# One Trainium2 core, a hybrid decoder block: the last chunk of y_b kept on chip and merged first, with its loads and splits in another order

## The chip, the core and the metric

The kernel runs on one core of a Trainium2 chip. TensorE (PE) multiplies, VectorE (DVE), ScalarE (ACT) and GpSimd (POOL) do elementwise work, and SyncE (SP) issues most of the transfers. Each engine takes its instructions in the order in which they were written for it, and waits at the first one whose data is not there. The metric is the device time of one execution in microseconds (us): the median of three runs of the kernel before is 2276.87 us (2275.35 to 2277.63).

## The reference

For an input x of 2048 positions by 1024 channels the block computes, in float32:

```
q, k, v, g_attn, u_lru, g_lru, gate_logits = split(x @ w_in + b_in)
y_a = (attention over 3 dilated head groups * silu(g_attn)) @ w_attn_proj
h   = rg_lru(conv(u_lru));   y_b = (h * silu(g_lru)) @ w_lru_proj
merged = sigmoid(gA) * y_a + sigmoid(gB) * y_b
out = layer_norm(2**0.25 * x + merged @ w_out + b_out)
```

The three attention groups are combined per head by their softmax denominators before the gate. Each product is made of three float32r products of split operands (high*high, high*low, low*high), so every operand is split into a rounded part (ACT) and a remainder (DVE, sometimes POOL) before PE reads it.

## The kernel before

All of w_in is multiplied first, then the attention runs. The change touches only what follows, from about 1792 us to the end. In that part the 2048 positions are four chunks of 512 columns (`c`), and the 1024 channels are eight blocks of 128 rows (`f`, `k`).

**y_b.** `yb_job(n)`, n = 0 to 31, goes through the chunks in order, eight output blocks each. One product is 24 matmuls of 128x512 (eight k, three products each). VectorE multiplies the result with its gate (`gB`, loaded by `load_gb` one product ahead) and SyncE stores it to DRAM (`yb_scr`). Around each product the loop places other work: the splits of w_lru_proj (`prep_wl`), of the next chunk's h (`load_h`, one block of the next chunk per product, so its block 7 is loaded in a chunk's last product and split in the next chunk's first), of w_attn_proj in the last chunk (`prep_wa`), and parts of W_out (`prep_wo`, 16 halves `(k, j)`: four at n = 16 to 19, four at n = 28 to 31).

**The combination.** `combine(c, hp)` joins the three attention groups for one chunk and one pair of heads: three loads (`oc`), weights on VectorE and ScalarE two products later, norms on VectorE and five tensor operations on GpSimd three products later, and four transposes on TensorE (`ctp`, one PSUM buffer) five products later, whose result VectorE multiplies into `ga`; it is stored to `at_scr`. The table `cmb` says behind which product each of the 16 stands: behind products 3 to 25, chunk 0 first.

**y_a and the output.** `ya_job(i)` multiplies the combined attention by w_attn_proj: 12 matmuls. VectorE multiplies the result with its gate (`gA`), and GpSimd adds the reloaded y_b (`ybr`) into `ME[c]`; both were loaded by `load_ya` two products ahead. The gates have three buffers (`gt`), so the load of gate i+3 waits until the addition of product i has read gate i. `out_job(tt)` multiplies 128 merged positions by W_out (two halves of 24 matmuls) and does the layer norm. It needs the split of `ME[c]`, which `split_m` makes, in three pieces for the first tile. The first eight y_a products carry the last eight halves of W_out, two with each of the products 0 to 3: each half is loaded behind its product and split (`later(1, ...)`) ahead of the next product's evacuation. After them come output tiles and y_a products of the next chunk in turn.

`later(lag, fn)` puts work off by so many products, and `run(late)` at a product's start writes what is due. Buffers are named slots: Z0 to Z2 and X0 to X5 of 16 KB per partition, `rc` six and `gt` three of 2 KB.

Of the kernel before, what the change touches and what calls it, by code (L numbers as in the profile page):

```python
# [15 lines left out]
P = 128  # L16
S = 2048
D = 1024
# [13 lines left out]
def hybrid_block_kernel(ctx: ExitStack, tc: tile.TileContext, a: dict, out: bass.AP):  # L32
# [1127 lines left out]
    GB = {}  # L1160

    def load_gb(n):
        c, f = divmod(n, 8)
        GB[n] = gt(f"gB{n}")
        sp.dma_start(GB[n], mg_scr[D + f * P:D + (f + 1) * P, c * CH:(c + 1) * CH])

    def yb_job(n):
        c, f = divmod(n, 8)
        cs = slice(c * CH, (c + 1) * CH)
        run(late)  # L1170
        if n + 1 < 32:
            load_gb(n + 1)
        yb = fp.tile([P, CH], F32, tag="y", name=f"yb{c}{f}", bufs=4)
        for k in range(8):
            xx = HH[c, k]
            pe.matmul(yb, WL[f][:, 0, k], xx[:, 0], start=(k == 0), stop=False)  # L1176
            pe.matmul(yb, WL[f][:, 0, k], xx[:, 1], start=False, stop=False)  # L1177
            pe.matmul(yb, WL[f][:, 1, k], xx[:, 0], start=False, stop=(k == 7))  # L1178
            if k == 3:
                run(pe_late)  # L1180
        gb = GB.pop(n)
        dve.scalar_tensor_tensor(out=gb, in0=gb, scalar=1.0, in1=yb, op0=ALU.add, op1=ALU.mult)
        later(1, lambda: sp.dma_start(yb_scr[f * P:(f + 1) * P, cs], gb))
        now["n"] += 1

    load_gb(0)
    for n in range(32):
        c, f = divmod(n, 8)
        if n < 6:
            prep_wl(n + 2)  # L1190
        if c + 1 < NCH:
            load_h(c + 1, f)
        else:
            prep_wa(f)
        if 16 <= n < 20 or n >= 28:
            prep_wo(*wo.pop(0))
        if 27 <= n < 31:
            load_at(0, n - 27)
        yb_job(n)
        if n in cmb:  # L1200
            combine(*cmb[n])
# [6 lines left out]


    vx_p = ctx.enter_context(tc.tile_pool(name="vx_p", bufs=1, reuse_waits="tile"))  # L1210
    vec = []
    for j in range(3):
        t = vx_p.tile([P, D], F32, name=f"vec{j}")
        sp.dma_start(t, a["vecs"][j:j + 1, :].broadcast_to([P, D]))
        vec.append(t)
    epst = cst.tile([P, 1], F32, name="epst")
    dve.memset(epst, EPS)

    ME, YG, XR, MS = {}, {}, {}, {}

    def load_ya(i):
        c, f = divmod(i, 8)
        cs = slice(c * CH, (c + 1) * CH)
        YG[i] = gt(f"gA{i}"), rc(f"ybr{i}")
        sp.dma_start(YG[i][0], mg_scr[f * P:(f + 1) * P, cs])
        sp.dma_start(YG[i][1], yb_scr[f * P:(f + 1) * P, cs])

    def ya_job(i):
        c, f = divmod(i, 8)
        if i + 2 < 32:  # L1230
            load_ya(i + 2)
        ga, yb = YG.pop(i)
        ya = fp.tile([P, CH], F32, tag="y", name=f"ya{c}{f}", bufs=4)
        for k in range(4):
            xx = AT[c][:, k]
            pe.matmul(ya, WA[f][:, 0, k], xx[:, 0], start=(k == 0), stop=False)
            pe.matmul(ya, WA[f][:, 0, k], xx[:, 1], start=False, stop=False)
            pe.matmul(ya, WA[f][:, 1, k], xx[:, 0], start=False, stop=(k == 3))
        if f == 0:
            ME[c] = big(("Z0", "Z1")[c % 2], [P, 8, CH], F32, f"me{c}")  # L1240
        dve.scalar_tensor_tensor(out=ga, in0=ga, scalar=1.0, in1=ya, op0=ALU.add, op1=ALU.mult)
        pool.tensor_tensor(out=ME[c][:, f], in0=ga, in1=yb, op=ALU.add)  # L1242

    def load_xr(tt):
        XR[tt] = vx_p.tile([P, D], F32, tag="x", name=f"x{tt}", bufs=3)
# [2 lines left out]
    def split_m(tt, ks=slice(0, 8)):  # L1248
        c, b = divmod(tt, 4)
        m = ME[c][:, ks, b * P:(b + 1) * P]  # L1250
        if ks.start == 0:
            MS[tt] = tuple(vx_p.tile([P, 8, P], F32R, tag=t, name=f"{t}{tt}", bufs=2) for t in ("mh", "ml"))
        mh, ml = (t[:, ks] for t in MS[tt])
        act.activation(mh, m, AF.Copy)
        dve.tensor_tensor(out=ml, in0=m, in1=flat(mh), op=ALU.subtract)

    def out_job(tt):
# [5 lines left out]
        for hf in range(2):  # L1263
# [5 lines left out]
                pe.matmul(z, mh[:, k], w[:, 1, hs], start=False, stop=False)  # L1269
                pe.matmul(z, ml[:, k], w[:, 0, hs], start=False, stop=(k == 7))  # L1270
            zz.append(z)
        if tt + 1 < 16:
            load_xr(tt + 1)
            split_m(tt + 1)
# [39 lines left out]
    def bring_at(c):  # L1314
        for k in range(4):
            if c < NCH:
                load_at(c, k)
        now["n"] += 1

    bring_at(1)  # L1320
    for tt in range(16):
        c, b = divmod(tt, 4)
        run(late)
        out_job(tt)
        if c + 1 < NCH:
# [64 lines left out]
```

## Time and profile before

| what | us |
|---|---|
| median of three runs (lowest, highest) | 2276.87 (2275.35, 2277.63) |
| the profiled execution's own time | 2272.4 |
| span of the profile | 2270.6 |
| first y_b matmul | 1792.1 |
| first y_a matmul | 1983.5 |
| first output matmul | 2013.5 |
| last output matmul | 2261.5 |

The profile is of one execution. Its page has the busy time of each engine, the span in 40 slices with the granted TensorE clock, the chain of work that ended last and the costliest groups of instructions. Its trace can be asked for stretches of time, for who waited for whom, and for single instructions with the idle time in front of them and what ended it. TensorE is busy for 98% of the span, so an edit shows in the time only where TensorE stands still.

### The profile page before, as it was taken

The page shows a single profiled execution, that of the slowest core. Times are in us where ns is not written, and L with a number is a line of the kernel's source. Part 1 is how long each engine was busy: PE and PEld are TensorE (multiplying, and loading weights), DVE is VectorE, ACT ScalarE, POOL GpSimd, SP SyncE. Part 2 cuts the span into 40 slices and gives each one's busy share as a digit, 9 for nine tenths or more (in the row PEclk, how much of TensorE's full clock was granted, in tenths as well). Part 3 has the DMA queues.
Part 4 walks back from the last instruction along what each step waited for, and adds up shares of the span by engine and source line. Part 5 has one row for each costly group of instructions (what it writes and reads, how often), then busy time and mean ns, then how long its engine had stood idle before and what let it go on. Part 6 is the DMA issues. An engine that isn't in the chain of part 4 may idle for free.

```text
span 2270.6 us, 33643 instructions
## 1 busy us (share of the span) xinstructions
PE 2218.0 (98%) x11032; PEld 1869.3 (82%) x11032; DVE 1748.2 (77%) x3244; ACT 1209.9 (53%) x2161; POOL 821.6 (36%) x606
## 2 busy tenths in 40 slices
PE   8999999999999999999999999989999999989998
PEld 6888888888887888888888888889999877767786
DVE  7888898899888786877888877656666578747677
ACT  5456566666565566766677677556666411221100
POOL 1555455455543001201201200476766156421220
PEclk9999999999999999999999999999999999999999
DMA  6977987977977666666766856996977588764431
GB/s 209 261 230 223 264 234 232 259 225 247 262 236 261 210 192 205 212 181 198 221 198 198 230 174 203 264 243 160 261 181 174 177 278 289 255 209 158 157 121 65
DMA packets 307358, 485.84 MB, mean 214 GB/s; under 512 B 90432, under 2 KB 131424, under 8 KB 302576
## 3 DMA queue, kind: packets, MB, share of 16 engines
q1 hardware_dynamic: 278192, 441.80, 63.1%
q0 software_dynamic: 9888, 17.90, 4.9%
q10 hardware_dynamic: 19104, 23.99, 3.4%
q8 instruction: 88, 1.44, 0.3%
q14 instruction: 86, 0.70, 0.1%
HBM read 305.27 MB, written 178.32 MB: 213 GB/s over the span
## 4 chain that ended last, share of the span: by engine, by line
PE 80%; issue 5%; DMA 5%; DVE 5%; POOL 3%; ACT 2%; SPq 1%; ACTq 0%; DVEq 0%; POOLq 0%
PE q L614 58%; PE o L988 4%; PE s L949 3%; PE yb L1177 2%; PE yb L1178 2%; PE yb L1176 2%; PE pt L964 2%; PE z L1270 1%; PE z L1269 1%; PE z L1268 1%; DMA A<-qh_scr 1%; POOL me L1242 1%; PE vtp L366 1%; DMA ybr<-yb_scr 1%; POOL C L797 1%
## 5 line engine op out<-in xcount | busy, mean ns | idle before, releaser
L614 PE MATMUL q<-xT,hS 128*128 128x512 f32 x1632 | 504.0, 390 | 1.4 <-DVE y L230 1.4
L614 PE MATMUL q<-xB,hA 128*128 128x512 f32 x1344 | 417.4, 392 | 9.5 <-ACT xB L218 8.8
L614 PE MATMUL q<-xT,l 128*128 128x512 f32 x1088 | 423.6, 389 | 0.0
L614 PE MATMUL q<-xB,l 128*128 128x512 f32 x944 | 368.4, 390 | 0.0
L614 PEld LDWEIGHTS q<-xT,hS 128*128 128x128 f32 x1632 | 305.3, 188 | 64.8 <-issue 1.8
L614 PEld LDWEIGHTS q<-xB,hA 128*128 128x128 f32 x1344 | 252.3, 189 | 62.9 <-ACT xB L218 8.8
L614 PEld LDWEIGHTS q<-xT,l 128*128 128x128 f32 x1088 | 204.2, 188 | 42.6
L955 ACT ACTIVATE p<-p,osb 128x256 f32<-128x256 f32 (+1 forms) x384 | 156.4, 454 | 112.4 <-DVE osb L953 109.2
L614 PEld LDWEIGHTS q<-xB,l 128*128 128x128 f32 x944 | 177.7, 188 | 37.2
L953 DVE CUSTOM_DVE_ANT_0 p<-s,mask 128x256 f32<-128x256 f32 (+1 forms) x384 | 125.3, 364 | 97.2 <-PE s L949 63.0
L230 POOL TENSOR_TENSOR sw<-sw,sin 128x512 f32<-128x512 f32 x96 | 154.6, 1632 | 122.6 <-ACT sw L318 99.8
L230 POOL TENSOR_TENSOR y<-y,h 128x512 f32<-128x512 f32 x28 | 40.3, 1440 | 413.7 <-DVE h L517 292.6
L988 PE MATMUL o<-V,ptb 128*128 128x65 f32 x1200 | 165.7, 276 | 9.5 <-ACT ptb L969 7.5
L988 PEld LDWEIGHTS o<-V,ptb 128*128 128x128 f32 x1200 | 152.7, 195 | 20.8 <-ACT ptb L969 18.2
L614 PE MATMUL q<-xB,hS 128*128 128x512 f32 x544 | 168.6, 391 | 0.3 <-DVE v L230 0.3
L614 PE MATMUL q<-xT,hA 128*128 128x512 f32 x544 | 168.2, 390 | 0.1
L274 ACT ACTIVATE hA<-wA 128x512 fp32r<-128x512 f32 x220 | 138.8, 635 | 21.2 <-PE g L483 6.6
L274 ACT ACTIVATE hS<-S 128x512 fp32r<-128x512 f32 x170 | 108.5, 638 | 63.8 <-DVE S L230 56.6
L230 POOL TENSOR_TENSOR l<-wA,hA 128x512 fp32r<-128x512 f32 x68 | 108.5, 1596 | 80.8 <-ACT hA L274 59.2
L949 PE MATMUL s<-B,A 128*128 128x256 f32 (+1 forms) x384 | 116.2, 325 | 4.1 <-DMA A<-qh_scr 2.1
L614 PEld LDWEIGHTS q<-xT,hA 128*128 128x128 f32 x544 | 101.6, 188 | 21.5 <-issue 0.7
L614 PEld LDWEIGHTS q<-xB,hS 128*128 128x128 f32 x544 | 101.3, 188 | 21.3 <-issue 0.7
(196 smaller groups left out, 4923.6 us busy)
## 6 DMA issues: line engine op xcount, KB each, us to landing
wA<-in_w_in_dram SPq DMA_DIRECT2D x219, 256.0 KB, 4.6
wl_scr<-l SPq DMA_DIRECT2D x102, 512.0 KB, 4.6
l<-wl_scr SPq DMA_DIRECT2D x102, 512.0 KB, 4.0
wS<-in_w_in_dram SPq DMA_DIRECT2D x102, 256.0 KB, 4.2
wS<-in_w_in_dram POOLq DMA_DIRECT2D x68, 256.0 KB, 6.8
mg_scr<-y SPq DMA_DIRECT2D x59, 256.0 KB, 5.0
o_scr<-osb ACTq DMA_DIRECT2D x48, 264.0 KB, 6.0
oc<-o_scr SPq DMA_DIRECT2D x48, 264.0 KB, 5.0
```

The costliest lines, as they stand in the source:

```text
L230: eng.tensor_tensor(out=out, in0=in0, in1=in1, op=op)
L274: act.activation(heads(h), heads(r, False), AF.Copy)
L366: pe.transpose(tp[:, b, :], flat(vt)[:, b * P:(b + 1) * P], ident)
L614: pe.matmul(bank, w[:, ks], x[:, kk, xx], start=(first and i == 0), stop=(last and i == 11))
L949: pe.matmul(s[:, h, (0 if g == 2 and n else lo):256], q, k, start=(i == 0), stop=(i == 1))
L953: dve.tensor_tensor_reduce(out=p[:, h, lo:256], in0=s[:, h, lo:256], in1=mask[:, lo:256], scale=1.0, scalar=3e38, op0=ALU.add, op1=ALU.min ...
L955: act.activation(p[:, h, lo:256], p[:, h, lo:256], AF.Exp, scale=-1.0, bias=mm)
L964: pe.transpose(pt[:, 2 * h + x, :], p[:, h, x * P:(x + 1) * P], ident)
L988: pe.matmul(o[:, n % 2, h * 65:h * 65 + 65], ptb[:, 2 * h + x, :], V[:, kb, vo + h * 65:vo + h * 65 + 65], start=(x == lo // P), stop=(x = ...
L1176: pe.matmul(yb, WL[f][:, 0, k], xx[:, 0], start=(k == 0), stop=False)
L1177: pe.matmul(yb, WL[f][:, 0, k], xx[:, 1], start=False, stop=False)
L1178: pe.matmul(yb, WL[f][:, 1, k], xx[:, 0], start=False, stop=(k == 7))
```

## The change

Eight things are done, all of them behind the attention:

- The combination takes chunk 3 first (order 3, 0, 1, 2) and is spread over products 2 to 27 (`cmb`).
- The y_a products and the output tiles take the chunks in that order too.
- In y_b's last chunk VectorE writes its gated result into `ME[3]` (a new slot, Z3) and it is not stored; the first eight y_a products add to it in place and load no `ybr`. In products 6 and 7 that addition is VectorE's, not GpSimd's.
- The gates of y_a's products 0 and 1 are loaded in y_b's products 30 and 31, and from product 23 on gates are loaded two products ahead.
- From chunk 1 on, `load_h` runs one block ahead: blocks 0 and 1 in a chunk's first product, none in its last.
- The last eight halves of W_out are loaded one per y_a product, over products 0 to 7.
- The three vectors of the norm and the first x tile, which were loaded before and after the first eight y_a products, are loaded behind products 3, 5, 6 and 4.
- The split of the merged tile lies in slot Z1, two halves in turn, in place of two buffers of `vx_p`.

```diff
-    cmb = {3 + (3 * i) // 2: divmod(i, 4) for i in range(16)}
+    CO = (3, 0, 1, 2)
+    cmb = {2 + (5 * i) // 3: (CO[i // 4], i % 4) for i in range(16)}
...
     def load_gb(n):
+        if n >= 32:
+            load_ya(n - 32)
+            return
...
-        if n + 1 < 32:
-            load_gb(n + 1)
+        for m in (n + 1,) if n < 23 else (n + 1, n + 2) if n == 23 else (n + 2,):
+            load_gb(m)
...
+        if c == CO[0]:
+            if f == 0:
+                ME[c] = big("Z3", [P, 8, CH], F32, f"me{c}")
+            dve.scalar_tensor_tensor(out=ME[c][:, f], in0=gb, scalar=1.0, in1=yb, op0=ALU.add, op1=ALU.mult)
+        else:
+            dve.scalar_tensor_tensor(out=gb, in0=gb, scalar=1.0, in1=yb, op0=ALU.add, op1=ALU.mult)
+            later(1, lambda: sp.dma_start(yb_scr[f * P:(f + 1) * P, cs], gb))
...
+    def load_ya(i):
+        c, f = CO[i // 8], i % 8
+        cs = slice(c * CH, (c + 1) * CH)
+        ga = gt(f"gA{i}")
+        sp.dma_start(ga, mg_scr[f * P:(f + 1) * P, cs])
+        yb = None
+        if c != CO[0]:
+            yb = rc(f"ybr{i}")
+            sp.dma_start(yb, yb_scr[f * P:(f + 1) * P, cs])
+        YG[i] = ga, yb
+
+    HL = {0: (0, 1), 7: ()}
...
-        if c + 1 < NCH:
+        if c == 0:
             load_h(c + 1, f)
+        elif c + 1 < NCH:
+            for k in HL.get(f, (f + 1,)):
+                load_h(c + 1, k)
...
     def ya_job(i):
-        c, f = divmod(i, 8)
+        c, f = CO[i // 8], i % 8
...
-        if f == 0:
-            ME[c] = big(("Z0", "Z1")[c % 2], [P, 8, CH], F32, f"me{c}")
+        if yb is None:
+            yb = ME[c][:, f]
+        elif f == 0:
+            ME[c] = big(("Z3", "Z0")[i // 8 % 2], [P, 8, CH], F32, f"me{c}")
         dve.scalar_tensor_tensor(out=ga, in0=ga, scalar=1.0, in1=ya, op0=ALU.add, op1=ALU.mult)
-        pool.tensor_tensor(out=ME[c][:, f], in0=ga, in1=yb, op=ALU.add)
+        (dve if i in (6, 7) else pool).tensor_tensor(out=ME[c][:, f], in0=ga, in1=yb, op=ALU.add)
+
+    ms = big("Z1", [P, 2, 2, 8, P], F32R, "ms")
+    TT = [4 * c + b for c in CO for b in range(4)]
...
-    load_ya(0)
-    load_ya(1)
     for i in range(8):
         run(late)
         ya_job(i)
         if wo:
             prep_wo(*wo.pop(0))
-        if wo:
-            prep_wo(*wo.pop(0))
+        if i in (3, 5, 6):
+            load_vec((i - 3) - (i > 4))
         if i == 4:
-            split_m(0, slice(0, 4))
+            load_xr(TT[0])
+            split_m(TT[0], slice(0, 4))
         if i == 6:
-            split_m(0, slice(4, 6))
+            split_m(TT[0], slice(4, 6))
         now["n"] += 1
     run(late)
-    split_m(0, slice(6, 8))
-    load_xr(0)
+    split_m(TT[0], slice(6, 8))
```

**VectorE where chunk 3 of y_b begins.** `hr37` is the raw last block of chunk 3's h, split into `h34`; `gB23` is the evacuation of the last product of chunk 2, `ga` that of a transposed combination; `cM`, `cE`, `cL` are a combination's weights and norms. Before:

```order
L1182 SCALAR_TENSOR_TENSOR gB23_19651<-gB23_19651,yb27_19699 128x512
...
L1110 TENSOR_TENSOR cE30_19624<-cE30_19624,cM30_19623 128x8 x3
L1093 TENSOR_TENSOR cM31_19683<-oc31_19679 128x8
L1094 TENSOR_TENSOR cM31_19683<-cM31_19683,oc31_19679 128x8
L1096 TENSOR_TENSOR cE31_19684<-cM31_19683,oc31_19679 128x8 x3
L1014 TENSOR_TENSOR h34_19506<-hr37_19686,h34_19506 128x512
```

Now:

```order
L1193 SCALAR_TENSOR_TENSOR gB22_19583<-gB22_19583,yb26_19624 128x512
...
L1110 TENSOR_TENSOR cE13_19556<-cE13_19556,cM13_19555 128x8 x3
L1014 TENSOR_TENSOR h34_19440<-hr37_19611,h34_19440 128x512
L1124 TENSOR_TENSOR ga12_19560<-ga12_19560,ctp12_19703 128x4x128
L1193 SCALAR_TENSOR_TENSOR gB23_19622<-gB23_19622,yb27_19690 128x512
```

The split of the last h block stood behind the evacuation of product 23, a norm and the next weights; it now stands one product earlier, ahead of that evacuation, and no weights stand in that product.

**SyncE in the first y_a products.** `gA` are the gates, `ybr` the reloaded y_b, `wor41` is half 1 of row block 4 of W_out, `vec0` a vector of the norm. Before:

```order
L1225 DMA gA2_20196<-mg_scr_72 128x512
L1226 DMA ybr2_20197<-yb_scr_73 128x512
L1147 DMA wor40_20217<-in_w_out_dram 128x512
L1147 DMA wor41_20219<-in_w_out_dram 128x512
L1225 DMA gA3_20225<-mg_scr_72 128x512
L1226 DMA ybr3_20226<-yb_scr_73 128x512
L1147 DMA wor50_20244<-in_w_out_dram 128x512
L1147 DMA wor51_20246<-in_w_out_dram 128x512
```

Now:

```order
L1125 DMA at_scr_70<-ga23_20064 128x512
L1203 DMA gA2_20183<-mg_scr_72 128x512
L1147 DMA wor40_20201<-in_w_out_dram 128x512
L1203 DMA gA3_20205<-mg_scr_72 128x512
L1147 DMA wor41_20222<-in_w_out_dram 128x512
L1203 DMA gA4_20226<-mg_scr_72 128x512
L1147 DMA wor50_20243<-in_w_out_dram 128x512
L1203 DMA gA5_20247<-mg_scr_72 128x512
L1147 DMA wor51_20264<-in_w_out_dram 128x512
L1242 DMA vec0_20177<-in_vecs_dram 128x1024
```

Four transfers per product became two, and each half of W_out still stands behind a gate; the halves go on to product 7.

**VectorE at the end of the first y_a products.** `ya07` and `ya37` are the results of product 7, `ms` and `ml` the split of the merged tile. Before:

```order
L1014 TENSOR_TENSOR wo6_20271<-wor71_20301,wo6_20271 128x512
L1241 SCALAR_TENSOR_TENSOR gA4_20252<-gA4_20252,ya04_20311 128x512
L1255 TENSOR_TENSOR ml0_20327<-me0_20213,mh0_20326 128x512
L1241 SCALAR_TENSOR_TENSOR gA5_20280<-gA5_20280,ya05_20334 128x512
L1241 SCALAR_TENSOR_TENSOR gA6_20307<-gA6_20307,ya06_20353 128x512
L1255 TENSOR_TENSOR ml0_20327<-me0_20213,mh0_20326 128x256
L1241 SCALAR_TENSOR_TENSOR gA7_20330<-gA7_20330,ya07_20374 128x512
L1255 TENSOR_TENSOR ml0_20327<-me0_20213,mh0_20326 128x256
```

Now:

```order
L1014 TENSOR_TENSOR wo6_20286<-wor61_20312,wo6_20286 128x512
L1262 SCALAR_TENSOR_TENSOR gA6_20269<-gA6_20269,ya36_20321 128x512
L1263 TENSOR_TENSOR me3_19767<-gA6_20269,me3_19767 128x512
L1279 TENSOR_TENSOR ms_20182<-me3_19767,ms_20182 128x256
L1014 TENSOR_TENSOR wo6_20286<-wor70_20336,wo6_20286 128x512
L1262 SCALAR_TENSOR_TENSOR gA7_20295<-gA7_20295,ya37_20347 128x512
L1263 TENSOR_TENSOR me3_19767<-gA7_20295,me3_19767 128x512
L1014 TENSOR_TENSOR wo6_20286<-wor71_20362,wo6_20286 128x512
L1279 TENSOR_TENSOR ms_20182<-me3_19767,ms_20182 128x256
```

The last four evacuations stood behind all splits of W_out; now each of them stands behind one, and the last piece of the merged tile behind the very last.

More of the change, by code (lines that the diff above doesn't have):

```diff
@@ L1210, in hybrid_block_kernel, with load_vec @@
     vx_p = ctx.enter_context(tc.tile_pool(name="vx_p", bufs=1, reuse_waits="tile"))
[L1211 to L1215, printed above, removed]
+    vec = [vx_p.tile([P, D], F32, name=f"vec{j}") for j in range(3)]
+    def load_vec(j):
+        sp.dma_start(vec[j], a["vecs"][j:j + 1, :].broadcast_to([P, D]))
     epst = cst.tile([P, 1], F32, name="epst")
     dve.memset(epst, EPS)
-    ME, YG, XR, MS = {}, {}, {}, {}
-    def load_ya(i):
-        c, f = divmod(i, 8)
[L1223 to L1226, printed above, removed]
     def ya_job(i):
-        c, f = divmod(i, 8)
+        c, f = CO[i // 8], i % 8
         if i + 2 < 32:
@@ L1251, in split_m @@
         if ks.start == 0:
-            MS[tt] = tuple(vx_p.tile([P, 8, P], F32R, tag=t, name=f"{t}{tt}", bufs=2) for t in ("mh", "ml"))
+            MS[tt] = ms[:, b % 2, 0], ms[:, b % 2, 1]
         mh, ml = (t[:, ks] for t in MS[tt])
@@ L1271, in out_job @@
             zz.append(z)
[L1272 to L1274 removed]
+        if tt != TT[-1]:
+            nx = TT[TT.index(tt) + 1]
+            load_xr(nx)
+            split_m(nx)
         st_ = cst.tile([P, 2, 6], F32, tag="st", name=f"st{tt}", bufs=2)
```

16 lines of the change are left out of this document (8 added, 8 removed).

## The prediction

> **What bounds the kernel now.** I read the chain of waits first, to see which engine sets the end, then the stretches from 1792 us on, which are all that the change touches, and then, for each stretch in which PE stood still, the rows of the engines it waited for.
>
> ```profile
> PE 80%; issue 5%; DMA 5%; DVE 5%; POOL 3%; ACT 2%; SPq 1%; ACTq 0%; DVEq 0%; POOLq 0%
> ```
>
> ```profile
> core 0: us, PE busy (x) PEld busy (x) DVE busy (x) ACT busy (x) POOL busy (x), PEclk, DMA share, GB/s
> 1792.10:1983.40 191.30, 185.53 (x834) 151.07 (x834) 140.67 (x374) 34.84 (x72) 97.76 (x80) 0.99 0.83 271
> 1983.40:2029.00 45.60, 37.39 (x146) 28.38 (x145) 15.05 (x24) 7.13 (x13) 10.54 (x8) 0.93 0.77 249
> 2029.00:2261.70 232.70, 229.84 (x1009) 188.67 (x1008) 166.88 (x279) 27.91 (x42) 37.09 (x24) 1.00 0.37 124
> ```
>
> PE sets the end. The three stretches are y_b, the first eight y_a products with the first output tile, and the rest. PE is idle for 5.8, 8.2 and 2.9 us there. The third stretch's 2.9 us lie at chunk borders that the change doesn't touch, so only the first two can pay. What PE waited for, in the groups of waits from 1792 us on (total, times, longest):
>
> ```profile
> PE ya L1236 <- DVE gA L1241: 4.9, 2, 4.1
> PE z L1270 <- DVE ml L1255: 3.7, 4, 1.3
> PE yb L1176 <- ACT h L1013: 3.2, 1, 3.2
> PE z L1268 <- ACT mh L1254: 2.3, 2, 2.0
> PE ctp L1119 <- issue: 1.2, 1, 1.2
> PE yb L1176 <- ACT wl L1016: 0.5, 1, 0.5
> PE yb L1178 <- DVE wl L1017: 0.3, 1, 0.3
> ```
>
> Row 3 is the block of h that a chunk's first product waits for, row 5 the transposes of a combination, rows 1, 2 and 4 the first y_a products and their output tile. The slower clock that follows a stall adds to them.
>
> **The change in y_b.** The one long wait is at chunk 3's begin, here in PE's, VectorE's and GpSimd's own order:
>
> ```profile
> 1936.80 0.39 PE L1178 MATMUL yb<-h,wl 128*128 128x512 f32 x1
> 1940.35 0.49 PE L1176 MATMUL yb<-h,wl 128*128 128x512 f32 x1 [3.17 <-ACT h L1013]
> 1941.26 0.50 PE L1177 MATMUL yb<-h,wl 128*128 128x512 f32 x1 [0.41 <-DVE h L1014]
> 1941.83 0.40 PE L1176 MATMUL yb<-h,wl 128*128 128x512 f32 x1
> 1942.06 0.40 PE L1177 MATMUL yb<-h,wl 128*128 128x512 f32 x1
> 1942.65 0.63 PE L1176 MATMUL yb<-h,wl 128*128 128x512 f32 x1
> 1943.07 0.63 PE L1177 MATMUL yb<-h,wl 128*128 128x512 f32 x1
> ```
>
> ```profile
> 1937.54 1.90 DVE L1096 TENSOR_TENSOR cE<-cM,oc 128x8 f32<-128x8 f32 x3
> 1940.33 0.87 DVE L1014 TENSOR_TENSOR h<-hr,h 128x512 fp32r<-128x512 f32 x1 [0.89 <-ACT h L1013]
> 1936.37 3.05 POOL L1112 TENSOR_TENSOR oc<-oc,cE 128x512 f32<-128x512 f32 x3 [3.52 <-DVE cM L1093]
> ```
>
> A matmul follows another after 0.23 us (1941.83 to 1942.06), at half clock after 0.43 (1942.65 to 1943.07). 1936.80 to 1940.35 instead of 0.23 is 3.32 us; 1940.35 to 1941.26 is 0.68 more; seven matmuls at 0.43 add 7 x 0.20 = 1.4. Together 5.4. The split of block 7 stands on VectorE behind a combination's weights, whose three small operations take 1.90 us beside GpSimd's 3.05. With blocks loaded one ahead, block 7 is split a product earlier: 24 x 0.227 = 5.44 us against a lateness of 3.3, so the wait goes, with 2.1 to spare: **+5.4**.
>
> The transposes' wait (1.2, and 0.2 for its restart) comes from one buffer being read late by VectorE; a combination every 5/3 products in place of 3/2 spaces them: **+1.4**. Against this, the early combinations now fall one product earlier, where w_lru_proj is still being split; PE lost 0.5 + 0.3 there to `wl` (rows 6 and 7), and I take **-0.3** more. The last combination's four transposes now follow the last product of y_b: at most four matmuls' time, 4 x 0.23 = 0.9, and since each has a quarter of the columns I take about half, **-0.4**. Sum for y_b 5.4 + 1.4 - 0.3 - 0.4 = **6.1**, from 4 (the transposes' wait stays and the early one doubles) to 7.
>
> Three edits here I cost at nothing. Writing the gated result into `ME[3]` is the same VectorE operation with another target, and eight stores of 256 KB go. The new slot Z3 pushes the raw loads of w_lru_proj onto memory that the attention reads: the first pair, issued at 1785.95, can only go out at about 1792.3, when the last attention product has read it. Behind it on SP stand the next pair, a block of h and a gate; product 2, the first that needs it, starts at 1792.1 + 2 x 5.44 = 1803.0, so some 6 us of PE work cover it. The gate loads that move two ahead wait on SP for an addition two products back instead of one; behind them stand loads of h and w_attn_proj that are due a product later.
>
> ```profile
> 1785.95 0.90 SPq L1026 DMA_DIRECT2D wlr<-in_w_f_dram  x2
> ```
>
> **The change in the first y_a products.** Before:
>
> ```profile
> 1983.46 0.39 PE L1236 MATMUL ya<-at,wa 128*128 128x512 f32 x1
> 1996.83 0.39 PE L1238 MATMUL ya<-at,wa 128*128 128x512 f32 x1
> 2001.31 0.80 PE L1236 MATMUL ya<-at,wa 128*128 128x512 f32 x1 [4.08 <-DVE gA L1241]
> 2022.04 0.50 PE L1268 MATMUL z<-wo,mh 128*128 128x512 f32 x1 [1.99 <-ACT mh L1254]
> 2028.99 0.39 PE L1236 MATMUL ya<-at,wa 128*128 128x512 f32 x1
> ```
>
> ```profile
> 1986.19 0.44 SPq L1225 DMA_DIRECT2D gA<-mg_scr  x1
> 1992.37 0.69 DVE L1241 SCALAR_TENSOR_TENSOR gA<-gA,ya 128x512 f32<-128x512 f32 x1 [6.81 <-DMA gA<-mg_scr]
> 1993.57 1.29 POOL L1242 TENSOR_TENSOR me<-gA,ybr 128x512 f32<-128x512 f32 x1 [20.85 <-DMA ybr<-yb_scr]
> 1994.89 0.33 SPq L1225 DMA_DIRECT2D gA<-mg_scr  x1
> 1998.69 1.24 ACT L1013 ACTIVATE wo<-wor 128x512 fp32r<-128x512 f32 x2 [17.51 <-DMA wor<-in_w_out_dram]
> 1999.35 1.30 DVE L1014 TENSOR_TENSOR wo<-wor,wo 128x512 fp32r<-128x512 f32 x2 [6.29 <-ACT wo L1013]
> 2000.57 0.68 DVE L1241 SCALAR_TENSOR_TENSOR gA<-gA,ya 128x512 f32<-128x512 f32 x1
> 2006.27 0.33 SPq L1225 DMA_DIRECT2D gA<-mg_scr  x1
> 2011.50 0.63 ACT L1013 ACTIVATE wo<-wor 128x512 fp32r<-128x512 f32 x1 [2.35 <-DMA wor<-in_w_out_dram]
> ```
>
> Gate 0 is issued after y_b and is there 8.9 us after the first matmul (1992.37 - 1983.46). Now it is there already, and evacuation 0 needs only the product, 2.7 us, and its own 0.7: some 6 us earlier. Not all of it reaches the end, because the rows show a loop. Evacuation 1 (2000.57) stands on VectorE behind a W_out split (1999.35), that behind ScalarE's (1998.69), that behind a half's landing; on SP the halves stand behind a gate load (1994.89), and this waits until GpSimd's addition (1993.57 + 1.29 = 1994.86) has freed a gate buffer. One lap carries two products, for which PE needs 5.44. With a half per product it is: addition end to gate issue 0.03; gate issue to half landed L; ScalarE 0.63; VectorE's split 0.69 (1.30 where GpSimd works); evacuation 0.69; GpSimd's addition 1.29; handoffs 0.2.
>
> For L there are bounds. The landing of `wor` from issue, 1984 to 2030 us, and the rate of a full stretch:
>
> ```profile
> DMA to landing us min/median/max: 2.9/4.2/8.3
> 2024.00:2028.00 4.00, 4.00 (x19) 3.33 (x18) 0.00 (x0) 0.00 (x0) 0.00 (x0) 1.00 1.04 403
> ```
>
> The least landing, with 0.3 for the gate's issue ahead of it and 0.65 for the gate's own 256 KB at 403 GB/s, is 2.9 + 0.3 + 0.65 = 3.85; gate 6, issued at 2006.27 in a group of four loads, had its half in ScalarE's hands at 2011.50, 5.2 later. The groups are now of two, so I take 3.85, and keep 5.3 for the range. Then a lap is 0.03 + 3.85 + 0.63 + 0.69 + 0.69 + 1.29 + 0.2 = 7.4, less what an uncovered split saves; I use 7.3. Before, the halves ended with product 3, so that two laps were slow; now they run through product 7: four.
>
> From the first y_a matmul, worked by hand with these durations: evacuation 0 ends at 3.7, its addition at 5.0; half 1 is split by 10.8 and addition 2 ends at 12.8; the even additions then follow each 7.3 us (20.1, 27.4), the odd ones at 10.9, 18.2 and 25.5. The last two are VectorE's, so no GpSimd step follows. Half 7 lands at about 30 in a group of three (its gate, a vector of 512 KB, itself), evacuation 7 ends at 32, its addition by 33, and the last split piece 0.6 later: PE starts on k = 6 of the first output tile at **33.6**. Before it was 2022.04 - 1983.46 = 38.6. That is **+5.0**.
>
> A new stall goes against it. PE reaches k = 6 at about 29 and stands for 4.6 us. After the 4.08 us before 2001.31 it ran at half clock:
>
> ```profile
> 2001.30:2007.00 5.70, 5.70 (x13) 4.46 (x14) 2.59 (x3) 1.15 (x2) 2.55 (x2) 0.50 0.61 172
> ```
>
> 13 matmuls in 5.70 us, 0.2 us each too long: **-2.6**. The wait for `at` behind the first tile (0.23 idle, 0.4 with its restart) should go, since it shares VectorE with fewer splits: **+0.4**. Sum for y_a 5.0 - 2.6 + 0.4 = **2.8**.
>
> [...]
>
> Costed at nothing here: the vectors and the first x tile, 2 MB, move from around these products into products 3 to 6, where they queue behind a half, not ahead of it, so that they meet the next gate and half only in part; a 512 KB load is 1.3 us of the rate above, and if it stood in full ahead of each half the four laps would lose up to 5.2. Reloads of y_b no longer lie between gate and half, which pays some of this. `ms` in Z1 is used two tiles in turn like the pair it replaces. The order of the chunks changes only which rows are read; at the later borders the additions and splits stand as before.
>
> **The rivals.**
>
> *The lap is heavier*: L is 5.3, as for gate 6. Four laps cost 4 x 1.45 = 5.8 more, gain 8.9 - 5.8 = 3.1, **2273.8**. For: the same pair of loads took that long, and 0.77 of the DMA engines' time was taken in this stretch. Against: fewer loads stand between.
>
> *The stall of y_b only moves*: VectorE, busy for 140.67 of 191.30 us, is late for another split and PE loses there what it won at block 7; only y_a's 2.8 is left, **2274.1**. Against: I find 2.1 us of spare at block 7.
>
> *The loop breaks*: gates and halves come early enough that PE never waits. Then 144 matmuls x 0.227 = 32.7 us lie from first y_a matmul to the end of the first tile, in place of 45.5; with the 0.4, y_a gains 13.2 and the whole 19.3, **2257.6**. Against: nothing that frees a gate buffer or moves a half ahead of a gate is in the change.
>
> *Slower*: the vectors and x get between gate and half, and each lap is set by a load that comes late. The decision point is L = 3.85 + (8.9 + 4.6) / 4 = 7.2; the longest landing of `wor` was 8.3. At 7.5 the four laps lose 14.6, **2282.6**. For: in this stretch such a load and a gate did delay one another (6.81 us of waiting for gate 0). Against: the median landing was 4.2.
>
> **How the numbers follow.** The profiled execution took 2272.4 us, 4.5 under the median of the three runs; I take gains as the same for both. 6.1 + 2.8 = 8.9: the profiled time becomes 2263.5 and the median 2276.87 - 8.9 = **2268.0**. Chances: forecast 0.55, heavier lap 0.22, moved stall 0.07, broken loop 0.08, slower 0.08. The forecast's own range is 2262 to 2273: y_b from 4 to 7, and L half a us either way (2.0). For 8 in 10 I go into the heavier lap and leave out most of the ends: **2260 to 2277**. 0.2%, about what a measurement of this kernel tells from no change, is 4.6 us; heavier lap and moved stall fall within it. Faster: 0.55 and 0.08, less a little of the forecast's edge, 0.62; same 0.29; slower 0.09.
>
> **What would show it.** Right: no wait of PE for `h` over 1 us at a chunk's first product; y_b's 32 products about 185 us long instead of 191.3; evacuation 0 of y_a within 4 us of the first y_a matmul; the gate loads from gate 3 on still issued just behind an addition, and the additions about 7.3 us apart in pairs; one stall of PE over 4 us ahead of `z` with half clock behind it. Wrong: a new wait for `h`, `wl` or `wa` in y_b; laps of 9 us or more; or no stall ahead of the first tile, in which case the gain is about twice what I say.

## The result, and the profile after

The change takes 2265.59 us (median of four runs, 2263.34 to 2267.38), the kernel before 2277.25 (2275.35 to 2279.47): ratio 0.9954, 95% interval 0.9941 to 0.9967, a gain of 7.5 to 13.4 us. The forecast was 2268.0.

The profiled execution of the change took 2267.4 us and its span is 2265.6. Single executions start the changed part at different times: over the fourteen profiled kernels of this case the first y_b matmul lies between 1790.7 and 1798.2 us, though all run the same work up to there. So stages are compared by their lengths. The windows of the change, cut at its own first y_b matmul, first y_a matmul and end of the first output tile:

```profile
core 0: us, PE busy (x) PEld busy (x) DVE busy (x) ACT busy (x) POOL busy (x), PEclk, DMA share, GB/s
1794.08:1978.60 184.52, 182.57 (x833) 150.01 (x833) 143.73 (x373) 34.27 (x72) 98.75 (x80) 1.00 0.85 277
1978.60:2025.10 46.50, 37.08 (x148) 29.25 (x146) 23.59 (x36) 10.74 (x17) 8.07 (x6) 0.85 0.62 198
2025.10:2256.70 231.60, 229.27 (x1009) 188.90 (x1008) 161.24 (x271) 24.08 (x37) 37.24 (x24) 1.00 0.36 123
```

y_b lost PE only 2 us of idle time in place of 5.8, and it is 6.8 us shorter. The middle stretch is not: 46.5 us against 45.6, with PE idle for 9.4 us and the clock at 0.85 in place of 0.93. The third is a little shorter. What PE waited for from 1792 us on:

```profile
PE z L1292 <- ACT ms L1278: 8.1, 2, 4.7
PE z L1294 <- DVE ms L1279: 3.7, 3, 1.3
PE ctp L1119 <- issue: 1.1, 1, 1.1
PE yb L1182 <- ACT wl L1016: 0.6, 1, 0.6
PE yb L1184 <- DVE wl L1017: 0.3, 1, 0.3
```

No row is left for `h` or for a `ya` product. All of the y_a stretch's waiting now stands ahead of the first output tile (row 1 and 1.3 us of row 2), where before it was spread. PE's rows there:

```profile
2006.80 0.50 PE L1292 MATMUL z<-wo,ms 128*128 128x512 f32 x1 [3.33 <-ACT ms L1278]
2008.88 0.79 PE L1294 MATMUL z<-wo,ms 128*128 128x512 f32 x1 [1.34 <-DVE ms L1279]
2015.69 0.80 PE L1292 MATMUL z<-wo,ms 128*128 128x512 f32 x1 [4.74 <-ACT ms L1278]
2016.28 0.63 PE L1293 MATMUL z<-wo,ms 128*128 128x512 f32 x1
2020.97 0.45 PE L1292 MATMUL z<-wo,ms 128*128 128x512 f32 x1
```

The tile's sum goes over eight row blocks `k`, 0 to 7; the first stall is for k = 4, the second for k = 6. From 2015.69 to 2020.97 PE runs at half clock. But the half clock did not begin with the second stall. The clock that the profile records as granted is half in one piece, from 0.6 us after PE had resumed from the first stall:

```profile
2007.44:2021.09 13.65, 7.57 (x18) 5.35 (x18) 6.98 (x13) 4.75 (x8) 0.00 (x0) 0.50 0.89 287
```

One lap of the y_a products, in the rows of GpSimd, SyncE, ScalarE and VectorE (addition 2, gate 5, half 3, evacuation 4, addition 4, gate 7):

```profile
1991.23 1.29 POOL L1263 TENSOR_TENSOR me<-gA,me 128x512 f32<-128x512 f32 x1 [1.23 <-DVE gA L1262]
...
1992.54 0.32 SPq L1203 DMA_DIRECT2D gA<-mg_scr  x1
1992.95 0.38 SPq L1147 DMA_DIRECT2D wor<-in_w_out_dram  x1
...
1997.29 0.63 ACT L1013 ACTIVATE wo<-wor 128x512 fp32r<-128x512 f32 x1 [2.53 <-DMA wor<-in_w_out_dram]
...
1997.96 0.69 DVE L1014 TENSOR_TENSOR wo<-wor,wo 128x512 fp32r<-128x512 f32 x1 [1.87 <-ACT wo L1013]
1998.57 0.68 DVE L1262 SCALAR_TENSOR_TENSOR gA<-gA,ya 128x512 f32<-128x512 f32 x1
...
1999.33 1.66 POOL L1263 TENSOR_TENSOR me<-gA,me 128x512 f32<-128x512 f32 x1 [1.88 <-DVE gA L1262]
...
2001.02 0.33 SPq L1203 DMA_DIRECT2D gA<-mg_scr  x1
```

The lap is there as forecast: the gate load goes out 0.02 us after the addition's end, the half behind it, then each engine waits for the one before. It took 8.5 us (1992.54 to 2001.02), of which L, from the gate's issue until ScalarE has the landed half, is 4.75.

### The profile page after: what moved, and what is told of

Same layout as the page of the kernel before. It is cut to its first block, busy times and chain, and to the rows that moved or that the text cites. A ratio compares the mean times of both kernels' runs of the same rounds, so it can differ in the third digit from the quotient of the medians.

```text
span 2265.6 us, 33610 instructions
## 1 busy us (share of the span) xinstructions
PE 2212.9 (98%) x11032; PEld 1867.7 (82%) x11032; DVE 1755.2 (77%) x3246; ACT 1209.0 (53%) x2161; POOL 819.4 (36%) x604
## 4 chain that ended last, share of the span: by engine, by line
PE 76%; DMA 8%; issue 5%; DVE 5%; POOL 3%; ACT 2%; SPq 1%; ACTq 0%; DVEq 0%; POOLq 0%
PE q L614 58%; PE o L988 3%; PE s L949 2%; DMA A<-qh_scr 2%; PE pt L964 1%; PE z L1294 1%; PE z L1293 1%; PE z L1292 1%; POOL C L797 1%; PE yb L1184 1%; DMA gB<-mg_scr 1%; PE yb L1182 1%; PE yb L1183 1%; PE vtp L366 1%; POOL me L1263 1%
## 5 line engine op out<-in xcount | busy, mean ns | idle before, releaser
L230 POOL TENSOR_TENSOR y<-y,h 128x512 f32<-128x512 f32 x28 | 40.3, 1438 | 414.4 <-DVE h L517 338.1
```

Source lines behind the costliest of these rows:

```text
L230: eng.tensor_tensor(out=out, in0=in0, in1=in1, op=op)
```

## The experiments

Each was timed in five rounds against the kernel before. The lengths below, in us, are, for each profiled execution, from the first y_b to the first y_a matmul, from there to the end of the first tile (where PE turns to the next chunk's y_a), and in brackets from the first y_a matmul to the tile's k = 6, all read from PE's own rows. Each length is of a single execution; the ratio is of all timed ones.

| kernel | y_b | first tile ends (k = 6) | ratio to before (95%) |
|---|---|---|---|
| before | 191.4 | 45.5 (38.6) | 1 |
| before, once more | 191.0 | 48.0 (39.6) | 0.9999 (0.9987 to 1.0011) |
| before, h ahead | 189.0 | 46.8 (39.9) | 0.9980 (0.9969 to 0.9990) |
| before, one combination moved | 186.3 | 48.9 (40.3) | 0.9980 (0.9972 to 0.9989) |
| before, combination spread | 183.6 | 48.3 (41.3) | 0.9972 (0.9961 to 0.9984) |
| the change | 184.6 | 46.4 (37.0) | 0.9954 (0.9941 to 0.9967) |
| the change, h not ahead | 183.7 | 46.0 (37.7) | 0.9952 (0.9940 to 0.9964) |
| the change, chunk 3 not kept | 192.3 | 60.8 (52.2) | 1.0060 (1.0046 to 1.0073) |
| the change, no vectors loaded | 184.7 | 44.0 (35.3) | 0.9948 (0.9935 to 0.9960) |
| the change, two halves per product | 184.7 | 38.8 (31.1) | 0.9925 (0.9911 to 0.9939) |
| the change, half before gate | 184.7 | 38.2 (29.9) | 0.9928 (0.9915 to 0.9941) |
| the change, gates in Z0 | 184.7 | 33.4 (26.2) | 0.9902 (0.9887 to 0.9917) |
| gates in Z0, two halves | 184.7 | 33.1 (26.1) | 0.9901 (0.9885 to 0.9917) |
| gates in Z0, h not ahead | 183.6 | 33.4 (26.2) | 0.9896 (0.9881 to 0.9912) |

**The kernel before, once more.** No edit.

> The kernel before, unchanged, as a measure of what two equal kernels differ by. Every theory: ratio 1.000, the interval within 0.15% of it. The profiled execution of the change gained 5.0 us on that of before, the medians 11.7, and the attention, which the change leaves alone, ended 2.0 us later in the profile of the change. If that is chance, the first y_b matmul here lies anywhere between 1790 and 1795 us, and the stretch from it to the first y_a matmul (191.4 us) and from there to the end of the first output tile (45.5 us) repeats within 0.5 us.

Ratio 0.9999; 2275.09 us, between 2272.33 and 2279.45. y_b repeats (191.0), the y_a stretch doesn't: 48.0 us against 45.5, and the first y_b matmul came at 1796.5, later than the 1790 to 1795 expected. The five profiled executions that keep the old y_a code have it between 45.5 and 48.9, 47.5 on average, so the profile of before shown ahead of the prediction had the best of them, and a comparison with it alone makes the change's y_a look worse (46.4) than it is.

**h one block ahead alone**, on the kernel before.

```diff
+    HL = {0: (0, 1), 7: ()}
...
-        if c + 1 < NCH:
+        if c == 0:
             load_h(c + 1, f)
+        elif c + 1 < NCH:
+            for k in HL.get(f, (f + 1,)):
+                load_h(c + 1, k)
```

> The kernel before with h one block ahead from chunk 1 on, and nothing else. Theory (the gain is made in y_b, most of it at chunk 3's begin): the wait for h of 3.3 us and the half clock after it go, y_b is 186 us long in place of 191.4, the time falls by 5.4 us, ratio 0.9976. Rival (VectorE is late for another split, the stall only moves): y_b stays at 190 us or more, ratio 0.999 to 1.001.

The wait for `h` is gone and y_b gains only 2.2 us, between the theory's 5.4 and the rival's 1.4 or less. The groups of PE's waits show where the rest went:

```profile
PE ctp L1119 <- issue: 3.3, 2, 2.7
PE yb L1176 <- ACT wl L1016: 0.5, 1, 0.5
PE yb L1178 <- DVE wl L1017: 0.3, 1, 0.3
```

The transposes wait 3.3 us in place of 1.2, once for 2.7, and half clock follows that wait (eight matmuls from 1920.54 to 1923.93, about 0.2 us too long each). VectorE, which has one split of `h` more to do in product 9, is later: counted from the first y_b matmul, it starts to read the transposes' one buffer (L1124) ahead of its evacuation of product 20 at 125.7 us, in the kernel before at 123.8, and that evacuation starts 2.0 us later (126.7 and 124.7). The next transposes start 0.1 us after the read's end, in both. The ratio of 0.998 leaves room for 2 to 7 us.

**The change with h not ahead.** The same lines put back in the change.

> The change with h loaded as before, one block per product and block 7 in a chunk's last product. With the kernel before, h ahead alone, and the change it makes a table of two by two for y_b: 191.2 us before, 189.0 with h ahead alone, 184.6 with h ahead and the spread combination. Theory (both edits together are needed, since either alone leaves VectorE late for the other's work): y_b 188 to 190 us, the time 4 to 5 us above the change, ratio to before 0.9975. Rival (with the combination spread no block of h is late any more, and h ahead is worth nothing on top): y_b 185 us and the change's time.

The rival was right, and more than right: y_b is 183.7 us, 0.9 shorter than with h ahead. PE's waits from y_b on:

```profile
PE z L1289 <- ACT ms L1275: 9.0, 2, 5.3
PE z L1291 <- DVE ms L1276: 2.5, 3, 1.2
PE yb L1182 <- ACT wl L1016: 0.6, 1, 0.6
PE yb L1184 <- DVE wl L1017: 0.3, 1, 0.3
```

Neither `h` nor `ctp` appears: the transposes' 1.1 us in the change come with h ahead and go with it.

**The spread combination alone**, on the kernel before, chunks in the old order.

```diff
-    cmb = {3 + (3 * i) // 2: divmod(i, 4) for i in range(16)}
+    cmb = {2 + (5 * i) // 3: divmod(i, 4) for i in range(16)}
```

> The kernel before with the combination behind products 2 to 27 (the change's table) in its old order of chunks, and nothing else: h as before, y_b stored, y_a as before. The change without h ahead had y_b at 183.7 us, with it at 184.6, so the theory is now that the spread combination alone makes y_b's gain and h ahead none. Theory: y_b 183.5 to 185 us in place of 191.2, the first output tile 45.5 to 48 us as before, ratio to before 0.9965 to 0.997. Rival (the order with chunk 3 first, or y_b kept on chip with its eight stores gone, has a part in it): y_b 187 us or more, ratio 0.998 or more.

y_b 183.6 us: one line makes all of y_b's gain, 7.6 us, without another order of chunks, without h ahead and with the eight stores still there. The y_a stretch took 48.3 us, 0.3 above what was expected of it. The ratio, 0.9972, is 4 to 9 us.

**One combination moved**, from behind product 22 to behind product 23, on the kernel before.

```diff
-    cmb = {3 + (3 * i) // 2: divmod(i, 4) for i in range(16)}
+    cmb = {3 + (3 * i) // 2 + (i == 13): divmod(i, 4) for i in range(16)}
```

> The kernel before with one of the 16 combinations, the one behind product 22, put behind product 23, and nothing else. In the kernel before the norm of one combination and the weights of the next fall into the same product, ahead of the split of h's block 7. Theory (this coincidence makes the wait at chunk 3's begin): with the weights a product later, block 7's split is there in time, the wait for h of 3.3 us and the half clock behind it go, y_b 185.5 to 187.5 us, ratio 0.998. Rival (VectorE's total work in these products is what is late, the stall appears at the next split or at the transposes): y_b 189 us or more, ratio 0.999 to 1.001.

y_b falls to 186.3. VectorE's rows at chunk 3's begin (of a combination's norm the last row, of the next one's weights the first two):

```profile
1937.38 0.32 DVE L1110 TENSOR_TENSOR cE<-cE,cM 128x8 f32<-128x8 f32 x3
1937.62 0.69 DVE L1014 TENSOR_TENSOR h<-hr,h 128x512 fp32r<-128x512 f32 x1
1938.22 1.08 DVE L1124 TENSOR_TENSOR ga<-ga,ctp 128x512 f32<-128x512 f32 x1
1939.30 0.69 DVE L1182 SCALAR_TENSOR_TENSOR gB<-gB,yb 128x512 f32<-128x512 f32 x1
1939.91 0.33 DVE L1093 TENSOR_TENSOR cM<-oc 128x8 f32<-128x8 f32 x1
1940.27 0.97 DVE L1094 TENSOR_TENSOR cM<-cM,oc 128x8 f32<-128x8 f32 x1
```

The split of block 7 (second row) now follows the norm at once; the weights (last two rows), which stood ahead of it before, come a product later. So the wait at chunk 3's begin was the meeting of one combination's norm and the next one's weights in one product, and 5 of the 7.6 us come from parting them at that one place. Most of the rest is the transposes' waits, which are still there here (1.3 and 0.5 us) and gone with the full spread.

**Chunk 3 of y_b not kept.** The change with its y_b stored and reloaded like the other chunks.

```diff
-        if c == CO[0]:
-            ...
-            dve.scalar_tensor_tensor(out=ME[c][:, f], in0=gb, scalar=1.0, in1=yb, op0=ALU.add, op1=ALU.mult)
-        else:
-            dve.scalar_tensor_tensor(out=gb, in0=gb, scalar=1.0, in1=yb, op0=ALU.add, op1=ALU.mult)
-            later(1, lambda: sp.dma_start(yb_scr[f * P:(f + 1) * P, cs], gb))
+        dve.scalar_tensor_tensor(out=gb, in0=gb, scalar=1.0, in1=yb, op0=ALU.add, op1=ALU.mult)
+        later(1, lambda: sp.dma_start(yb_scr[f * P:(f + 1) * P, cs], gb))
...
-        yb = None
-        if c != CO[0]:
-            yb = rc(f"ybr{i}")
-            sp.dma_start(yb, yb_scr[f * P:(f + 1) * P, cs])
+        yb = rc(f"ybr{i}")
+        sp.dma_start(yb, yb_scr[f * P:(f + 1) * P, cs])
...
-        if yb is None:
-            yb = ME[c][:, f]
-        elif f == 0:
+        if f == 0:
```

> The change with y_b's chunk 3 stored to DRAM and reloaded like the other chunks, all else kept. Each gate load of the first y_a products has a reload of y_b behind it on SyncE again, ahead of the W_out half. Theory (what the kept chunk is worth is the shorter lap): the half is issued 0.4 us later and lands behind 256 KB more, so that a lap grows by 0.5 to 1 us, four laps by 2 to 4; the first tile ends 48.5 to 50.5 us behind the first y_a matmul in place of 46.4; y_b stays at 184.6; ratio to before 0.9965. Rival (the 256 KB are hidden behind the lap's other steps, and keeping the chunk pays nothing here): the first tile within 1 us of 46.4, ratio 0.995.

Both were far off: it is slower than the kernel before, y_b 7.7 and the first tile 14.4 us longer than in the change. SyncE's waits, 1935 to 2020 us, and the row of PE where y_b ends:

```profile
SPq L1171 <- DMA yb_scr<-gB: 32.6, 7, 6.6
SPq L1198 <- DMA yb_scr<-gB: 10.6, 3, 5.1
SPq L1198 <- POOL me L1254: 7.0, 3, 5.2
```

```profile
1988.19 1.09 PE L1119 MATMUL ctp<-ident,oc 128*128 128x128 f32 x4 [7.04 <-issue]
```

A gate loaded two products ahead takes the buffer of the product just before, and here that product's store must have read it first. SyncE stands at the gate load for that, 10 times for 43 us in all, with the loads of w_attn_proj, W_out and the combined attention behind it; they come late (from 1975 us on ScalarE waits 5.2 to 6.8 us for each load of w_attn_proj but the first), VectorE with them (2.7 to 6.1 us), and PE stands for 7 us before y_b's last transposes. In the change, SyncE waits for such a store once in the same stretch (6.8 us). By these waits the two edits belong together: without the kept chunk the rest of the change takes 22 us more. No run has the chunk not kept and the gates one product ahead, so how much of the 22 us is the gates' alone stays open.

**No vectors loaded.** The change without the 1.5 MB of the norm's vectors between the y_a products.

```diff
-        sp.dma_start(vec[j], a["vecs"][j:j + 1, :].broadcast_to([P, D]))
+        pool.memset(vec[j], 0.5)
...
+    for j in range(3):
+        load_vec(j)
...
-        if i in (3, 5, 6):
-            load_vec((i - 3) - (i > 4))
```

> The change without the loads of the three norm vectors: they are filled with a constant on GpSimd before the first y_a product, so the output is not the reference's; the first x tile is still loaded. It asks how much of the lap is the 1.5 MB that the change moved between the first y_a products' loads. In the profile of the change a half landed 3.7 us after its issue without a vector or x beside it and 4.1 to 5.3 us with one. Theory (they share the DMA engines with the half and stretch each lap): every half lands after 3.7 to 4.1, the last three laps shrink by 0.5 to 1 us each, k = 6 of the first tile starts 35 us behind the first y_a matmul in place of 37.0 and the time falls by 1.5 to 2.5 us, ratio to before 0.9945. Rival (the landing is what it is without them): within 0.5 us of the change.

k = 6 comes at 35.3 and the first tile ends 2.4 us earlier; the times (0.9948 against 0.9954) can't tell the two apart. The landing of the W_out halves around these products, first in the change and then here:

```profile
DMA to landing us min/median/max: 3.6/4.2/5.3
```

```profile
DMA to landing us min/median/max: 3.6/4.1/4.5
```

The longest landing fell by 0.8 and the least is still 3.6. Of the 3.4 us by which k = 6 came later than forecast (37.0, not 33.6) the vectors make about half, as far as one execution of each can tell (h not ahead, which has the change's y_a code, had 37.7); the other half is there without them.

**Two halves per product**, as before, in the rest of the change.

```diff
-        if wo:
-            prep_wo(*wo.pop(0))
+        for _ in range(2):
+            if wo:
+                prep_wo(*wo.pop(0))
```

> The change with the last eight W_out halves put back to two with each of the products 0 to 3. Theory (a lap of gate load, half, split, evacuation, addition sets the first y_a products wherever a half is split, and spreading the halves over eight products doubled the slow laps): two slow laps of 8.5 to 9.5 us, then products at their own pace; PE reaches k = 6 of the first tile at about 30 us behind the first y_a matmul in place of 37.0, and the time falls by 5 to 7 us against the change. Rival (the bytes that must be there by the first tile set its time, in whatever order): first tile at 36 us or later, no gain.

k = 6 at 31.1, the first tile 7.6 us earlier, 0.9925: some 6.6 us under the change. That is the gain that the theory had from halves up to product 3 only, two slow laps in place of four. How long a lap was here is not shown; a half took 3.9 to 6.0 us to land, in the change 3.6 to 5.3. This edit of the change, one half per product, made the kernel slower.

**The half before the gate.** One half per product, but its load is written ahead of the product's gate load.

```diff
+        if wo:
+            prep_wo(*wo.pop(0))
         ya_job(i)
-        if wo:
-            prep_wo(*wo.pop(0))
```

> The change with each W_out half loaded ahead of its product's gate on SyncE in place of behind it. Theory (the half's landing stands behind a gate load that waits for an addition): half i no longer waits for addition i-1 but for addition i-2, the lap of about 8 us carries three products in place of two, 2.7 us a product, which is PE's own pace; k = 6 of the first tile starts 30 to 32 us behind the first y_a matmul in place of 37.0, the time falls by 4 to 7 us against the change. Rival (the order on SyncE does not matter, the DMA engines' load does): within 1 us of the change.

k = 6 at 29.9, about the 30 to 32 expected, the first tile 8.2 us earlier, 0.9928. The bytes and their number are the same; only what they stand behind on SyncE is another.

**Gates in Z0.** The six gates of products 2 to 7 get slices of a slot that is free there, so that no gate load waits for an addition.

```diff
-        ga = gt(f"gA{i}")
+        if 2 <= i < 8:
+            if i == 2:
+                YG["t"] = big("Z0", [P, 8, CH], F32, "gz")
+            ga = YG["t"][:, i]
+        else:
+            ga = gt(f"gA{i}")
```

> The change with the gates of y_a's products 2 to 7 loaded into slot Z0, which is free from y_b's end until product 8, in place of three buffers in turn. No gate load waits for an addition any more, so the lap is gone while the halves stay one per product. Theory (the lap sets the first y_a products): PE reaches k = 6 of the first tile at its own pace, 27 to 30 us behind the first y_a matmul in place of 37.0, the first tile ends at 33 to 36 in place of 46.4, and the time falls by 10 to 13 us against the change, ratio to before 0.990. Rival (the transfers themselves or VectorE are the limit): the first tile ends at 41 us or later.

The first tile ends 33.4 us behind the first y_a matmul, 13.0 earlier than in the change; 2252.47 us, 0.9902. PE's waits and the halves' landing:

```profile
PE z L1299 <- DVE ms L1284: 2.4, 2, 1.3
PE ctp L1119 <- issue: 1.1, 1, 1.1
PE yb L1182 <- ACT wl L1016: 0.6, 1, 0.6
PE yb L1184 <- DVE wl L1017: 0.3, 1, 0.3
```

```profile
DMA to landing us min/median/max: 4.1/6.4/7.1
```

The y_a stretch has no wait left (row 1 is the later chunk borders), though a half takes 6.4 us to land in place of 4.2: the eight halves now go out within 15.0 us (1978.9 to 1993.9), in the change within 26.5 (1982.9 to 2009.4). Here the landing time by itself did not count; that it stood in a loop did.

**Gates in Z0, and two halves per product.** Both edits.

> Gates in Z0 and two W_out halves with each of the products 0 to 3. Theory: with the lap gone the number of halves per product no longer matters as long as the last half is split before PE reaches it; the first tile ends 33 to 35 us behind the first y_a matmul, within 1.5 us of the run with one half per product. Rival (VectorE and ScalarE are late with two splits per product): 1.5 us or more above that run.

33.1 us against 33.4, 0.9901 against 0.9902: with the loop open the number of halves per product doesn't matter.

**Gates in Z0, h not ahead.** The version that the findings point to.

> The change with the gates of products 2 to 7 in Z0 and with h loaded as before, not ahead. Theory: y_b 183.7 us as in the change without h ahead, the first tile ends 33.4 us behind the first y_a matmul as with the gates in Z0, so the stretch from the first y_b matmul to the end of the first tile is 217.1 us in place of 236.5 before; ratio to before 0.990, 1 us under the run with gates in Z0, which its interval won't tell. Rival (with the lap gone VectorE has h's last block late): y_b above 185.5 us.

2250.67 us, ratio 0.9896 (0.9881 to 0.9912), y_b 183.6 and the first tile 33.4. It beats the kernel before by 1.0% and the change by about 0.6%. From the two versions ahead of it the times can't tell it; only y_b's length, 183.6 against 184.7, does.

## Why the prediction was right, and where its steps were not

The time and its sign came as forecast: 2265.59 against 2268.0. From the traces, y_b's gain is 6.6 us (191.2 on average to 184.6), the first y_a products' 1.1 (47.5 on average to 46.4), and the rest's about 0.3 (231.5 to 231.2): 8 us, against 8.9 forecast and 7.5 to 13.4 measured. Only y_b's gain is clear of what single executions differ by; 1.1 lies inside the 45.5 to 48.9 of the old y_a code, and against the profile that the forecast used, y_a lost 0.9. The stages account for the low part of the interval; what might lie above that isn't assigned to anything. That a sum with one term right for a wrong reason and one mostly missing came within 2.4 us of the median is in part luck.

*y_b, 6.1 forecast, 6.6 measured, for the wrong reason.* The step that failed is the 5.4 put on "with blocks loaded one ahead, block 7 is split a product earlier". The wait had been read rightly: the split stands behind a combination's weights (1.90 us, beside 3.05 of GpSimd's). With h ahead alone the wait does go, but only 2.2 of the 5.4 are gained. But the spread table, priced at 1.4 for the transposes alone, moves those weights out of that product, and does it without h ahead: 7.6 us alone. h ahead gains so little alone because the transposes then wait longer (3.3 us, not 1.2), and on top of the spread it is worth -0.9. So the two terms did not add up as independent ones; the quoted row of 1.90 us for the weights named the cure, and the table was not laid over it. What the wait costs was right: 5.4 forecast, 4.9 when one moved combination takes it away. The transposes' 1.4 did not come in the change, where they still wait 1.1.

*The early products, -0.3, and the last transposes, -0.4.* No loss came: `wl` costs 0.6 + 0.3 in place of 0.5 + 0.3, and a wait of 0.2 for `h` at 1842 went. The last combination's four transposes take 0.35 us behind y_b's last product (1978.35 to 1978.70); before, they took the same 0.35 inside y_b (1974.83 to 1975.18), so moving them costs nothing.

*The edits at nothing.* Z3's later loads were covered as said: there is no wait for `wl` at product 2. By SyncE's waits, gate loads two ahead cost nothing here because chunk 3 isn't stored. The sum gave no price to "eight stores of 256 KB go"; a store takes a gate buffer away until it has landed (43 us of SyncE's waits in ten gate loads with chunk 3 stored, one wait of 6.8 us in the change), and without the kept chunk the kernel is 22 us slower.

*The first y_a products.* The loop was named rightly, as three edits that break it in three ways show (the first tile ends 8 to 13 us earlier). Its size was wrong in one term: L, taken as 3.85, was 4.1, 4.75, 4.7, 4.8 and 5.0 in the laps, and the last half, in a group of three:

```profile
2008.51 0.33 SPq L1203 DMA_DIRECT2D gA<-mg_scr  x1
2008.93 0.38 SPq L1207 DMA_DIRECT2D ybr<-yb_scr  x1
2009.41 0.38 SPq L1147 DMA_DIRECT2D wor<-in_w_out_dram  x1
```

```profile
2014.70 0.63 ACT L1013 ACTIVATE wo<-wor 128x512 fp32r<-128x512 f32 x1 [3.58 <-DMA wor<-in_w_out_dram]
2015.23 0.40 ACT L1278 ACTIVATE ms<-me 128x256 fp32r<-128x256 f32 x1
```

was 6.2 behind its gate load and held up the last piece of the first tile's split, which stands behind it on ScalarE. Laps took 7.4 to 8.5 us, not 7.3, and k = 6 came at 37.0, not 33.6. The forecast also had half 7 landed at about 30. It stands behind gate 9, which waits for addition 6, and that was forecast at 27.4: with the forecast's own L of 3.85 the half could not land before 31.3. Addition 6 ended at 29.8 and the half was there at 36.0. (The row that the forecast calls gate 6, issued at 2006.27, is gate 5's; the reading of 5.2 us stands.) The least landing was 2.9 before; here it was 3.6, and half of the rest came from the vectors, which the forecast had costed at nothing. The half clock was priced at 2.6 and cost 2.5 (46.4 - 37.0 = 9.4 us for what took 6.95 at full clock). That the size came out is luck: the half clock began at 2007.44, behind the stall of 3.33 us at k = 4, which the sum left out, and with h not ahead, where the second stall was longer (5.3 us), the same work lost only some 1.3 (46.0 - 37.7 = 8.3). The stall at k = 4 delayed nothing else, since k = 6 was later still. Evacuation 0 ended 3.9 us behind the first y_a matmul (3.7 forecast), and the wait for `at` behind the first tile went, as said.

*The rivals.* The heavier lap came in about halfway (L between 3.85 and 5.3); y_b's half us above its forecast paid for a part of it. The moved stall is what h ahead alone does. The loop breaks only with an edit that the change doesn't have; its price was right: 32.7 us forecast for the stretch, 33.4 with the gates in Z0. Its 2257.6 for the median was 5 us too high against 2252.47. The slower case needed L above 7.2; the longest was 6.2.

## What to carry to other kernels

Before pricing a wait by the edit that is aimed at it, lay every edit of the change over the rows that make it: here a table that spread some other work removed it, and the edit that was aimed at it cost time. Where a load waits for a consumer and another load stands behind it on the same queue, look for the loop and count the products in a lap: order on the queue, number of buffers, or fewer laps each made the first tile end 8 to 13 us earlier here, taking the vectors out of the loop's way 2.4. A buffer that is loaded further ahead must also be free earlier; ask which store still reads it.

## What the runs showed of the hardware

The same y_a code took 45.5 to 48.9 us in five profiled executions, and over all fourteen y_b began up to 7.5 us apart, so a single profile can't price a stage of transfers within 3 us. y_b repeated within 0.4 in two executions of the kernel before, and within 0.1 in six that have the change's y_b.

From y_b on, every one of the eleven stalls of PE of 4 us or more in the fourteen profiles had half clock behind it: 5.3 us of it (2015.69 to 2020.97) behind 4.74 in the change, 5.7 us behind 4.08 before, and 2.7 us (2018.21 to 2020.93) behind 5.30 with h not ahead. Shorter stalls had it too, and the stall next to the slow matmuls need not be the one behind which the half clock began: in the change the granted clock was half from 2007.44 on, behind a stall of 3.33 us, and the matmuls behind the stall of 4.74 lie in that same stretch. By PE's rows half clock came behind a stall of 2.73 us with h ahead alone, and behind one of 2.02 us in the kernel before, once more (matmuls 0.43 us apart from 2016.54 to 2019.95), while behind a stall of 2.02 us with one combination moved, which ended at 2008.45, the matmuls were 0.23 us apart from the second on. In the profile of before, the granted clock was half for 3.41 us (1942.37 to 1945.78) and 6.83 us (2000.40 to 2007.22) between the first y_b matmul and the last output matmul, in that of the change for 13.65 us (2007.44 to 2021.09).
